# A sixth buffer for split weights and six more 7-product row pairs in a decoder trunk

## The chip, the cores and the metric

The kernel runs on one core of one Trainium2 chip. The core has TensorE for matmuls (PE in the profile, with its weight loads shown apart as PEld), VectorE (DVE), ScalarE (ACT), GpSimd (POOL) and SyncE (SP, which here only issues transfers). The metric is the device time of one execution in microseconds, the median of several runs; lower is better.

## The reference

The model is a trunk of two layers over 256 tokens of width 2048. The first layer is RetNet retention with 8 heads, the second DeepSeek-style latent attention with 16 heads on one shared key and value; each is followed by an MLP with a squared ReLU and an inner width of 8192. Everything is float32.

```python
def sq_relu_mlp(h, w1, w2):
    return jnp.square(jax.nn.relu(h @ w1)) @ w2

x = x + retention(rms_norm(x, norm_mix[0]), ...)
x = x + sq_relu_mlp(rms_norm(x, norm_mlp[0]), mlp_w1[0], mlp_w2[0])
k_nope, k_pe, v = mla_shared_kv(rms_norm(x, kv_norm_in), ...)
x = x + mla_attention(rms_norm(x, norm_mix[1]), ..., k_nope, k_pe, v, ...)
x = x + sq_relu_mlp(rms_norm(x, norm_mlp[1]), mlp_w1[1], mlp_w2[1])
```

The weights of the two MLPs are four matrices of 64 MB each, more than half of all that is read.

## The kernel before

**Split products.** TensorE multiplies a rounded float32 form. To keep the precision, each operand is split into a high part (`wh` for weights, a cast on ScalarE, line 216) and a low part (`wl`, a subtraction on VectorE, line 217), and one product of blocks is three matmuls: high x high, high x low, low x high (lines 409 to 411). So every weight passes through ScalarE and VectorE before TensorE can use it. High and low parts have 5 buffers each, of 1024 columns.

**Row pairs and column pairs.** The matrices of the MLPs, the output projections and most of retention's are read in pieces of 1 MB, each a 2x2 of blocks: 256 rows (a row pair) by 1024 columns (a column pair). `gemm_pair` walks over the 8 row pairs of one column pair and adds into PSUM; `quad` does one row pair. A row pair is multiplied in one of two ways, chosen by the list `kinds`:

- with 8 products (the plain way): two high and two low parts of 1024 columns;
- with 7 products (a Strassen-Winograd form): VectorE first makes three sums u1 to u4 of the weight blocks (lines 363, 372 and 373), and then the blocks b11, b22, b21 and the sums are split into four high and four low parts, one of them half as wide. The activation side needs sums too, made by `with_sums` (lines 451 to 460) and held in a second activation tile, `more`. The sums of the results come out in `pair_out`.

The raw weights lie in 3 buffers (`raw`). A load is issued by SP as soon as the last reader of a buffer is done. In a row pair of 7 the last reader of the raw weights is the low part of b21, the second of its four low parts.

**The MLP.** `mlp` goes through 4 groups of 2048 hidden columns. A group has two column pairs of w1 (tiles `u_...`, results through `up`: ReLU, transposes on TensorE, square, split, and `with_sums` for 4 of its 8 hidden blocks) and two column pairs of w2 (tiles `d_...`). Results of w2 of groups 0 to 2 are added to x in device memory: `to_home` issues 8 accumulating transfers of 256 KB from GpSimd's queue, spaced out over the next column pair. The last group brings x back. Which row pairs have 7 products: in the first column pair of w1 of groups 1 to 3 it is `ODD` (1, 3, 5, 7), in the second `SEVEN` (3, 5, 7); in w2 `SEVEN` and then `ODD`.

**Order.** Program order comes from a queue: `later(n, fn)` puts work off by n ticks (one tick is one row pair), and `queued_behind` fixes the order of two instructions on their engine. The compiler's scheduler orders the rest, so an instruction can be issued before an earlier one of the program that waits for more. Each engine then issues its own list strictly in order, and waits on semaphores. Tiles come from pools with a fixed number of buffers for a tag; a tile whose buffers are all in use waits for the last reader of one. The activation tiles (`act`, 24 buffers) are all in use in a group: 12 of the layer's input (8 blocks and 4 `more`), 12 of the hidden blocks.

## Time and profile before

| | us |
|---|---|
| median of 3 runs | 2459.61 (2458.16 to 2460.76) |
| the profiled execution | 2458.1 |
| its span, from the first to the last instruction | 2456.3 |
| PE busy, PEld busy | 2446.2, 2057.6 |
| DVE busy | 2212.2 |
| ACT busy | 1641.3 |
| POOL busy | 238.0 |

The granted TensorE clock is 1.00 over the whole span. The first MLP runs from 721 to 1402 us, the second from 1774 to 2452 us. Matmuls overlap, so that each shows about 0.39 us of length while they start about 0.23 us apart; TensorE's pace is read from starts and counts, not from lengths. In the rows of the profile a group is named by line, engine, operation and its tiles, output<-input, with the numbers of tiles left out. "Idle before" is the time the engine stood still ahead of an instruction, with what ended that time.

### The profile page before, as it was taken

Reading aid. Unit: us, or ns where it says so; the run is one execution under the profiler, and the core shown is the slowest. Engines: PE = TensorE matmul, PEld = TensorE weight load, DVE = VectorE, ACT = ScalarE, POOL = GpSimd, SP = SyncE. Lnnn points to the kernel's source line nnn. Section 1 sums busy time; section 2 is a strip of 40 time slices with the busy share of each in tenths; the row PEclk is TensorE's granted clock in tenths of the full one; section 3 lists DMA queues with packets and bytes.
Section 4 is the critical chain, followed back from the end, with each engine's and each line's share of the span. In section 5 each row is a group of like instructions: output and inputs, shape, how many; then the busy total and the mean of one; then the engine's idle time right before and its main releaser. Section 6 shows DMA issues by size and latency. Waiting matters only on the chain.

```text
span 2456.3 us, 31721 instructions
## 1 busy us (share of the span) xinstructions
PE 2446.2 (100%) x11614; PEld 2057.6 (84%) x11614; DVE 2212.2 (90%) x2919; ACT 1641.3 (67%) x2307; POOL 238.0 (10%) x287
## 2 busy tenths in 40 slices
PE   9999999999999999999999999999999999999999
PEld 7888888888888888888888888998888888888887
DVE  7899899888899999999999998777899999999998
ACT  6566666556676767667676777577667667676674
POOL 6400001000000010010110001101000100100100
PEclk9999999999999999999999999999999999999999
DMA  8555569556565586695786555444555865957854
GB/s 309 207 201 191 192 202 259 191 183 224 197 218 194 196 254 218 207 272 187 241 253 213 200 202 180 155 162 173 197 199 205 252 228 194 262 198 229 264 209 170
DMA packets 93692, 521.05 MB, mean 212 GB/s; under 512 B 11104, under 2 KB 12512, under 8 KB 40288
## 3 DMA queue, kind: packets, MB, share of 16 engines
q1 hardware_dynamic: 72144, 472.83, 55.2%
q0 software_dynamic: 21248, 46.15, 8.9%
q8 instruction: 91, 1.49, 0.2%
q14 instruction: 65, 0.53, 0.1%
q10 hardware_dynamic: 144, 0.05, 0.0%
HBM read 479.14 MB, written 39.85 MB: 211 GB/s over the span
## 4 chain that ended last, share of the span: by engine, by line
PE 92%; DVE 2%; ACT 1%; issue 0%; DMA 0%; POOL 0%; ACTq 0%; DVEq 0%
PE u_c L411 7%; PE u_c L410 7%; PE u_c L409 7%; PE d_c L411 6%; PE d_c L410 6%; PE d_c L409 6%; PE rp_c L411 3%; PE rp_c L409 3%; PE rp_c L410 3%; PE u_p L411 2%; PE u_p L410 2%; PE u_p L409 2%; PE rq_acc L307 2%; PE rk_acc L307 2%; PE ro_c L411 2%; PE ro_c L409 2%
## 5 line engine op out<-in xcount | busy, mean ns | idle before, releaser
L217 DVE TENSOR_TENSOR d_wl<-d_raw,d_wh 128x1024 fp32r<-128x1024 f32 (+1 forms) x256 | 278.7, 1111 | 31.6 <-ACT d_wh L216 31.6
L217 DVE TENSOR_TENSOR u_wl<-u_raw,u_wh 128x1024 fp32r<-128x1024 f32 (+1 forms) x256 | 279.3, 1113 | 29.8 <-ACT u_wh L216 29.8
L409 PE MATMUL u_c<-u_wh,n 128*128 128x512 f32 x712 | 278.3, 392 | 0.0
L411 PE MATMUL u_c<-u_wh,n 128*128 128x512 f32 x712 | 277.2, 389 | 0.0
L410 PE MATMUL u_c<-u_wl,n 128*128 128x512 f32 x712 | 277.2, 389 | 0.0
L409 PE MATMUL d_c<-d_wh,hid 128*128 128x512 f32 x706 | 275.4, 392 | 0.5 <-ACT d_wh L216 0.5
L411 PE MATMUL d_c<-d_wh,hid 128*128 128x512 f32 x706 | 275.0, 390 | 0.0
L410 PE MATMUL d_c<-d_wl,hid 128*128 128x512 f32 x706 | 274.8, 389 | 0.0
L216 ACT CAST u_wh<-u_raw 128x1024 fp32r<-128x1024 f32 (+1 forms) x256 | 241.3, 973 | 49.6 <-PE u_c L411 24.1
L216 ACT CAST d_wh<-d_raw 128x1024 fp32r<-128x1024 f32 (+1 forms) x256 | 240.3, 971 | 39.9 <-PE d_c L411 16.6
L216 ACT CAST d_wh<-d_u 128x1024 fp32r<-128x1024 f32 x106 | 108.1, 1051 | 119.7 <-DVE d_u L373 82.6
L216 ACT CAST u_wh<-u_u 128x1024 fp32r<-128x1024 f32 x104 | 106.2, 1052 | 116.0 <-DVE u_u L373 77.3
L411 PEld LDWEIGHTS u_c<-u_wh,n 128*128 128x128 f32 x712 | 133.7, 188 | 27.8
L410 PEld LDWEIGHTS u_c<-u_wl,n 128*128 128x128 f32 x712 | 133.8, 188 | 27.4 <-DVE u_wl L217 0.3
L409 PEld LDWEIGHTS u_c<-u_wh,n 128*128 128x128 f32 x712 | 133.7, 188 | 27.0
L409 PEld LDWEIGHTS d_c<-d_wh,hid 128*128 128x128 f32 x706 | 132.6, 188 | 28.2 <-ACT d_wh L216 1.4
L411 PEld LDWEIGHTS d_c<-d_wh,hid 128*128 128x128 f32 x706 | 132.5, 188 | 27.6
L410 PEld LDWEIGHTS d_c<-d_wl,hid 128*128 128x128 f32 x706 | 132.6, 188 | 27.5 <-DVE d_wl L217 0.4
L216 ACT CAST rp_wh<-rp_raw 128x1024 fp32r<-128x1024 f32 x112 | 103.8, 945 | 74.2 <-PE rp_c L411 49.2
L217 DVE TENSOR_TENSOR rp_wl<-rp_raw,rp_wh 128x1024 fp32r<-128x1024 f32 x112 | 119.7, 1090 | 16.4 <-ACT rp_wh L216 16.2
L217 DVE TENSOR_TENSOR u_wl<-u_u,u_wh 128x1024 fp32r<-128x1024 f32 x104 | 123.5, 1222 | 3.1 <-ACT u_wh L216 2.8
L217 DVE TENSOR_TENSOR d_wl<-d_u,d_wh 128x1024 fp32r<-128x1024 f32 x106 | 125.8, 1221 | 0.0
(570 smaller groups left out, 6505.3 us busy)
## 6 DMA issues: line engine op xcount, KB each, us to landing
u_raw<-in_mlp_w SPq DMA_DIRECT2D x128, 1024.0 KB, 5.4
d_raw<-in_mlp_w SPq DMA_DIRECT2D x128, 1024.0 KB, 4.9
rp_raw<-in_ret_w_gv SPq DMA_DIRECT2D x56, 1024.0 KB, 4.8
ro_raw<-in_ret_w_out SPq DMA_DIRECT2D x32, 1024.0 KB, 4.9
uq_raw<-in_mla_w_uq SPq DMA_DIRECT2D x24, 768.0 KB, 4.3
rq_raw<-in_ret_w_qk SPq DMA_DIRECT2D x16, 1024.0 KB, 4.9
rk_raw<-in_ret_w_qk SPq DMA_DIRECT2D x16, 1024.0 KB, 4.8
xh<-d_c POOLq DMA_DIRECT2D x48, 256.0 KB, 6.1
```

Source lines behind the costliest of these rows:

```text
L216: nc.scalar.copy(h, src)
L217: return nc.vector.tensor_tensor(l, src, h.bitcast(F32), op=ALU.subtract)
L307: nc.tensor.matmul(acc[f], wh[:, cols], a.rearrange("p i s -> p (i s)"), start=k == 0, stop=k == nk - 1)
L409: nc.tensor.matmul(dst, ah, bh, start=n == 0, stop=False)
L410: nc.tensor.matmul(dst, ah, bl, start=False, stop=False)
L411: nc.tensor.matmul(dst, al, bh, start=False, stop=n == total[key] - 1)
```

## The change

- The high and the low parts get 6 buffers each.
- In groups 1 to 3 of both MLPs the first column pair of w1 has 5 row pairs with 7 products (`FIVE`: 1, 3, 5, 6, 7), taken in the order 0, 1, 3, 2, 5, 4, 6, 7. The sums of activation block 6, which nothing held so far, are made again from its high and low part by `sum_again`, during the second column pair of w2 of the group before, and held in a `more` tile.
- The space comes from several places: in a row pair of 7, u2 and u4 are summed in place in the raw weights, so that one `us` buffer is left of two; the parts of u1 and u3 now come before those of u2 and u4; the mask is cut to two blocks; the rope frequencies and gains come by loads of their own into a shared buffer when they are needed, not with the constants; the rope tables and the rotated key share two buffers; `small` has 26 buffers, not 36.

```diff
-            wh = pool.tile([P, 1024], F32R, tag="wh", bufs=5, name=f"{name}_wh{half}")
-            wl = pool.tile([P, 1024], F32R, tag="wl", bufs=5, name=f"{name}_wl{half}")
+            wh = pool.tile([P, 1024], F32R, tag="wh", bufs=6, name=f"{name}_wh{half}")
+            wl = pool.tile([P, 1024], F32R, tag="wl", bufs=6, name=f"{name}_wl{half}")
...
-        u = [pool.tile([P, 2, 512], F32, tag="us", bufs=2, name=f"{name}_u{i}") for i in range(2)]
+        u = pool.tile([P, 2, 512], F32, tag="us", bufs=1, name=f"{name}_u")
...
-        nc.vector.tensor_tensor(u[1][:, 0], u[0][:, 0], raw[:, 512:1024], op=ALU.add)
-        summed_up = nc.vector.tensor_tensor(u[1][:, 1], u[1][:, 0], raw[:, 1536:], op=ALU.add)
+        summed_up = nc.vector.tensor_tensor(raw[:, 1024:1536], u[:, 0], raw[:, 512:1024], op=ALU.add)
         b11, b22 = parts(raw[:, 0:1024], 2, 0, summed_up)
         mm("p1", a(0, 0), b11)
         mm("c12", s(3), b22)
         (b21,) = parts(raw[:, 1536:], 1, 1, summed_up)
         mm("c11", a(0, 1), b21)
-        u2, u4 = parts(u[1].rearrange("p i n -> p (i n)"), 2, 2)
+        last_sum = nc.vector.tensor_tensor(raw[:, 1536:], raw[:, 1024:1536], raw[:, 1536:], op=ALU.add)
+        queued_behind(last_sum, low_part[0])
+        u1, u3 = parts(u.rearrange("p i n -> p (i n)"), 2, 3, last_sum)
+        mm("p5", s(1), u1)
+        mm("p7", s(0), u3)
+        u2, u4 = parts(raw[:, 1024:], 2, 2)
         mm("c21", a(1, 1), u4)
         mm("p6", s(2), u2)
-        u1, u3 = parts(u[0].rearrange("p i n -> p (i n)"), 2, 3)
-        mm("p5", s(1), u1)
-        mm("p7", s(0), u3)
...
-    rope_tab = pool.tile([P, 2, S], F32, name="rope_tab")
-    pe_tabs = [[pool.tile([P, 2, ROPE], F32, name=f"petab{t}{i}") for i in range(2)] for t in range(NT)]
+    rope_tab = pool.tile([P, 2, S], F32, tag="tab", bufs=2, name="rope_tab")
+    pe_tab = pool.tile([P, NT, 2, 2, ROPE], F32, tag="tab", bufs=2, name="pe_tab")
+    pe_tabs = [[pe_tab[:, t, i] for i in range(2)] for t in range(NT)]
...
+    def inverse(lo, n, name):
+        inv = f2k([n], name)
+        nc.sync.dma_start(inv, a["cst"][:, lo : lo + n])
+        return inv
+
     def mla_tables():
+        gpe = f2k([2 * ROPE], "gpe")
+        nc.sync.dma_start(gpe, a["gpe"])
...
-        ret_sc.append(sincos(cst[:, C_INVR : C_INVR + 128], 128, "tr"))
+        ret_sc.append(sincos(inverse(C_INVR, 128, "invr"), 128, "tr"))
...
-            nc.sync.dma_start(cst, a["cst"])
-            nc.sync.dma_start(gpe, a["gpe"])
+            nc.sync.dma_start(cst, a["cst"][:, C_MASK:])
...
+        def sum_again(name):
+            v = act[6][0]
+            u = f2k([2, S], f"{name}_u")
+            nc.vector.tensor_tensor(u, v[:, :, 0].bitcast(F32), v[:, :, 1].bitcast(F32), op=ALU.add)
+            again[:] = [*act[:6], (v, with_sums(u, name)), act[7]]
...
-                seven = SEVEN if p % 2 else ODD if p else LATE
+                seven = SEVEN if p % 2 else FIVE if p else LATE
                 gemm_pair(
-                    w1, p * 8, act, [i in seven for i in range(8)], f"u{layer}_{p}", lambda c, p=p, up=up: up(c, p)
+                    w1, p * 8, again if p % 2 == 0 and p else act, [i in seven for i in range(8)], f"u{layer}_{p}",
+                    lambda c, p=p, up=up: up(c, p), order=(0, 1, 3, 2, 5, 4, 6, 7) if seven is FIVE else None,
                 )
...
+                if p and not last:
+                    later(4, lambda gi=gi: sum_again(f"n{layer}{gi}"))
+
```

More of the change, by code (lines that the diff above doesn't have):

```diff
@@ L47 @@
 SEVEN, LATE, ODD, HEAD = (3, 5, 7), (5, 7), (1, 3, 5, 7), (2, 4, 6, 7)
+FIVE = (1, 3, 5, 6, 7)
 QUERY, FOUR = (3, 4, 6, 7), (3, 5, 6, 7)
@@ L75, in small @@
     def small(w, name):
-        return pool.tile([P, w], F32, tag="small", bufs=36, name=name)
+        return pool.tile([P, w], F32, tag="small", bufs=26, name=name)
     def shaped(t, shape):
@@ L115, in yoco @@
     gains = pool.tile([P, G_ALL], F32, name="gains")
-    cst = pool.tile([P, C_ALL], F32, name="cst")
+    cst = pool.tile([P, C_ALL - C_MASK], F32, name="cst")
     pos_i = pool.tile([P, NT], I32, name="pos_i")
-    gpe = pool.tile([P, 2 * ROPE], F32, name="gpe")
     nc.scalar.dma_start(gains, a["gains"])
-    ident = cst[:, C_ID : C_ID + P]
-    mask = cst[:, C_MASK : C_MASK + 3 * P]
-    neg_half = pool.tile([P, 16], F32, name="neg_half")
+    mask = cst[:, 0 : 2 * P]
+    ident = cst[:, 2 * P : 3 * P]
+    neg_half = pool.tile([P, 8], F32, name="neg_half")
     nc.gpsimd.memset(neg_half, -0.5)
@@ L333, in parts @@
         def parts(src, n, part, after=None):
-            wh = pool.tile([P, 1024], F32R, tag="wh", bufs=5, name=f"{name}_wh{part}")
-            wl = pool.tile([P, 1024], F32R, tag="wl", bufs=5, name=f"{name}_wl{part}")
+            wh = pool.tile([P, 1024], F32R, tag="wh", bufs=6, name=f"{name}_wh{part}")
+            wl = pool.tile([P, 1024], F32R, tag="wl", bufs=6, name=f"{name}_wl{part}")
             low = low_part[0] = split(wh[:, : n * 512], wl[:, : n * 512], src)
@@ L695, in start @@
             later(6, scale_tables)
-            later(18, lambda: mla_sc.append(sincos(cst[:, C_INVM : C_INVM + 32], 32, "tm")))
+            later(18, lambda: mla_sc.append(sincos(inverse(C_INVM, 32, "invm"), 32, "tm")))
             later(26, mla_tables)
@@ L942, in yoco @@
     rc, ckv = [], []
-    kpe_t = pool.tile([P, 2, S], F32R, name="kpe_t")
+    kpe_t = pool.tile([P, 2, S], F32R, tag="tab", bufs=2, name="kpe_t")
     def downed(acc, b):
@@ L1225, in _constants @@
     causal = np.where(i[None, :] <= i[:, None], 0.0, -1e30)
-    cst[:, C_MASK : C_MASK + 3 * P] = np.concatenate([causal, np.zeros((P, P)), causal], axis=1)
+    cst[:, C_MASK : C_MASK + 2 * P] = np.concatenate([np.zeros((P, P)), causal], axis=1)
     cst[:, C_ID : C_ID + P] = np.eye(P)
```

7 lines of the change are left out of this document (4 added, 3 removed).

## The prediction

> **What bounds the kernel now.** I read the busy lines of the page first, then what TensorE waits for, then tables by stage, and last the timelines of VectorE and TensorE in one stage.
>
> ```profile
> span 2456.3 us, 31721 instructions
> PE 2446.2 (100%) x11614; PEld 2057.6 (84%) x11614; DVE 2212.2 (90%) x2919; ACT 1641.3 (67%) x2307; POOL 238.0 (10%) x287
> ```
> ```profile
> PE idle L131 <- DVE zeros L128: 1.2, 1, 1.2
> PE rg_acc L279 <- ACT a L218: 0.7, 1, 0.7
> ...
> PE d_c L409 <- ACT d_wh L216: 0.5, 2, 0.3
> ```
>
> TensorE is busy for 100% of the span, and its waits are tenths of a microsecond at a handful of places. VectorE is second with 90%. So one removed matmul is worth its full pace, and one added VectorE instruction is free only while VectorE stays ahead. The table by stage shows how far ahead. Its rows are one group of the first MLP: the second column pair of w2 of group 0 ("d, second"), the two column pairs of w1 of group 1 ("u, first" and "u, second"), and the first of w2 ("d, first"). Columns: window, its length, then busy time and instructions of PE, PEld, DVE, ACT and POOL, granted clock, DMA share, GB/s.
>
> ```profile
> 851.90:892.70 40.80, 40.80 (x181) 33.80 (x180) 37.49 (x41) 25.55 (x31) 6.96 (x8) 1.00 0.89 257
> 892.70:933.50 40.80, 40.80 (x181) 33.80 (x180) 37.06 (x41) 25.47 (x31) 6.90 (x8) 1.00 0.90 257
> 933.50:976.80 43.30, 43.30 (x201) 36.03 (x200) 40.95 (x52) 31.61 (x43) 0.00 (x0) 1.00 0.55 195
> 976.80:1020.10 43.30, 43.30 (x201) 36.04 (x200) 41.40 (x52) 31.62 (x43) 0.00 (x0) 1.00 0.55 194
> ```
>
> TensorE is never idle there, at clock 1.00. "u, first" has 4 row pairs of 7 products and 4 of 8, so (4x7 + 4x8) x 3 = 180 matmuls in 40.80 us: **0.227 us a matmul**. VectorE's idle time is 3.31, 3.74, 2.35 and 1.90 us, 11.30 us a group. What it waits for in this layer and in the second one (engine, line, us in total, times, longest):
>
> ```profile
> DVE u_wl L217 <- ACT u_wh L216: 10.4, 10, 1.8
> DVE u_u L363 <- DMA u_raw<-in_mlp_w: 4.0, 3, 2.0
> DVE d_u L363 <- DMA d_raw<-in_mlp_w: 3.9, 3, 2.1
> ```
> ```profile
> DVE u_u L363 <- DMA u_raw<-in_mlp_w: 2.1, 2, 1.5
> DVE d_u L363 <- DMA d_raw<-in_mlp_w: 0.3, 1, 0.3
> ```
> The timelines of VectorE, ScalarE and TensorE in "u, first" (start, length, instruction, idle before it):
> ```profile
> 889.72 1.23 DVE L217 TENSOR_TENSOR u_wl<-u_raw,u_wh 128x1024 fp32r<-128x1024 f32 x1 [1.57 <-ACT u_wh L216]
> ...
> 898.47 2.36 DVE L217 TENSOR_TENSOR u_wl<-u_u,u_wh 128x1024 fp32r<-128x1024 f32 x2
> 900.74 2.36 DVE L217 TENSOR_TENSOR u_wl<-u_raw,u_wh 128x1024 fp32r<-128x1024 f32 x2
> 903.01 1.22 DVE L363 TENSOR_TENSOR u_u<-u_raw 128x1024 f32<-128x1024 f32 x1
> ...
> 909.68 1.23 DVE L217 TENSOR_TENSOR u_wl<-u_raw,u_wh 128x1024 fp32r<-128x1024 f32 x1
> 912.91 1.23 DVE L363 TENSOR_TENSOR u_u<-u_raw 128x1024 f32<-128x1024 f32 x1 [2.01 <-DMA u_raw<-in_mlp_w]
> ...
> 927.00 2.35 DVE L217 TENSOR_TENSOR u_wl<-u_u,u_wh 128x1024 fp32r<-128x1024 f32 x2
> 930.51 1.23 DVE L217 TENSOR_TENSOR u_wl<-u_raw,u_wh 128x1024 fp32r<-128x1024 f32 x1 [1.16 <-ACT u_wh L216]
> ```
> ```profile
> 905.79 2.00 ACT L216 CAST u_wh<-u_u 128x1024 fp32r<-128x1024 f32 x2 [3.43 <-PE u_c L411]
> ```
> ```profile
> 900.41 0.39 PE L410 MATMUL u_c<-u_wl,n 128*128 128x512 f32 x1
> ...
> 932.37 0.39 PE L410 MATMUL u_p<-u_wl,n_more 128*128 128x512 f32 x1
> ```
> ```profile
> L217 DVE TENSOR_TENSOR u_wl<-u_u,u_wh 128x1024 fp32r<-128x1024 f32 x104 | 123.5, 1222 | 3.1 <-ACT u_wh L216 2.8
> ```
>
> Three readings. (1) VectorE's lead over TensorE is small: the first of the two low parts from 898.47 lasts 1.22 us, ends at 899.69 and is used at 900.41 (lead 0.72 us); the second of the two from 927.00 ends at 929.35 and is used at 932.37 (3.02 us). (2) Part of its idle time is a full buffer: the 1.57 us before 889.72 end with a ScalarE cast, and such casts wait for TensorE to free a high part (the 3.43 us before 905.79). (3) The rest is weights that land late: 2.01 us before 912.91.
>
> **The change part by part.**
>
> *Fifth row pair of 7 products.* Six column pairs (2 layers, groups 1 to 3) lose one product of 3 matmuls: 18 x 0.227 = **-4.08 us**. On VectorE a row pair of 8 costs two low parts, 903.01 - 900.74 = 2.27 us; one of 7 costs three sums and four low parts, 909.68 - 903.01 = 6.67 us. The swap adds 4.40 us of VectorE per column pair, which itself becomes 0.68 us shorter.
>
> *Sums of row pair 6, made again* (one 512-wide sum, the three of `with_sums`, a cast and a low part), in "d, second" of each group before:
>
> ```profile
> L373 DVE TENSOR_TENSOR u_u<-u_u,u_raw 128x512 f32<-128x512 f32 x4 | 2.8, 690 | 0.1
> ```
> ```profile
> L455 DVE TENSOR_TENSOR hid_sum<-hid_u x32: 418/422/429, 773.6 to 2379.4; 128x256 f32<-128x256 f32 x32
> ```
> ```profile
> L456 DVE TENSOR_TENSOR hid_sum<-hid_sum,hid_u x32: 284/292/297, 775.1 to 2381.6; 128x128 f32<-128x128 f32 x32
> ```
>
> The third of `with_sums` and the low part have the widths of the second and of the 512-wide sum: 0.69 + 0.42 + 0.29 + 0.29 + 0.69 = 2.38 us of VectorE. It has 3.31 us idle in that stage, so I put it at nothing; without that cover it costs up to 2.38 us x 6 = 14.3 us. Its cast goes to ScalarE, idle for 15.25 of the 40.80 us. The 25th activation tile that it needs takes the place of a hidden block that "d, second" has read by then; no wait expected.
>
> *Does VectorE still keep up?* A group had 11.30 us idle; 4.40 + 2.38 + 0.68 = 7.46 go, and 3.84 us stay. In the two critical stages in a row ("d, second", "u, first") 7.05 us were idle and 7.46 are wanted: 0.41 us too few, to be taken from the lead. If late weights stay as late as now, they take (4.0 + 3.9) / 3 = 2.6 us a group more in the first layer, and 0.8 us in the second. So the lead must give 0.4 to 3.0 us per group, and is rebuilt in the two stages after, which keep 4.25 us idle less what the next item takes.
>
> *Sixth buffer of high and low parts.* It gives room of one part, 6 to 12 matmuls, 1.36 to 2.72 us: what VectorE idles for a full buffer (1.57 us before 889.72) becomes lead. With the smallest lead shown, 0.72, some 2.1 to 3.4 us can be given. That covers 0.4 and 0.8 + 0.4, and 3.0 only with the larger gain. I price the stalls of the six stages at **0**, with bounds 0 and 2.3 us per group (the second case in the rivals).
>
> *New order inside every row pair of 7*: u1 and u3 go to TensorE before u2 and u4, which are now summed in place in the weights' own buffer. VectorE does the same three sums. Two prices are not in the trace. First, the last sum is now followed by its cast and only one low part covers that cast: cast 1.00 us of the 2.00 us pair at 905.79 plus two hand-overs against a low part of 1.13, so between 0 and about 0.2 us of VectorE per row pair; I take 0.05, since the next row pair's first sum can be put there, and up to 9 x 0.2 = 1.8 us in the two critical stages for the range. Second, the weights' buffer is freed only after the last low part, two low parts or 2.3 us later than now, and loads of "u, first" already land late.
>
> ```profile
> u_raw<-in_mlp_w SPq DMA_DIRECT2D x128, 1024.0 KB, 5.4
> ...
> xh<-d_c POOLq DMA_DIRECT2D x48, 256.0 KB, 6.1
> ```
>
> A load takes 5.4 us at the median, beside eight 256 KB accumulating transfers of POOL in each critical stage (DMA share 0.89 to 0.90 against 0.55 in the other two). Three weight buffers leave a load the time of two row pairs, 2.27 + 6.67 = 8.9 us at VectorE's full pace, so the median load is in time and a doubly shared one is not. I keep the waits as they are now; lower bound none, upper 2.0 us in each of the 12 critical stages.
>
> *What a sixth buffer may do elsewhere.* TensorE idles a little near the ends of both MLPs and in the projections between:
>
> ```profile
> 1356.40:1402.00 45.60, 44.98 (x203) 36.19 (x202) 44.65 (x65) 31.80 (x52) 2.44 (x5) 1.00 0.51 182
> 1402.00:1431.00 29.00, 28.52 (x212) 27.59 (x212) 21.78 (x46) 22.94 (x53) 3.80 (x6) 1.00 0.64 224
> 1431.00:1474.00 43.00, 42.76 (x193) 34.90 (x192) 42.36 (x62) 30.15 (x47) 2.20 (x1) 1.00 0.59 207
> ...
> 2409.00:2452.00 43.00, 42.29 (x184) 33.98 (x182) 41.50 (x51) 19.55 (x23) 0.00 (x0) 1.00 0.48 159
> ```
>
> 0.62 + 0.48 + 0.24 + 0.71 = 2.05 us idle. VectorE is nearly full there (44.65 of 45.60), so more room helps only with what was done ahead; bounds 0 and -2.05, I take half: **-1.0**.
>
> *Space made for it.* The constants' load is split: the frequencies come by a load of their own just before the tables, the rope gains much later. POOL starts its chain for the tables later by the landing of that load; bounds 0 and one load of 5.4 us:
>
> ```profile
> 18.15 1.55 POOL L570 TENSOR_SCALAR tr_ang<-cst,pos_f 128x128 f32<-128x128 f32 x2 [17.31 <-DVE pos_f L628]
> ...
> 59.55 0.73 POOL L206 TENSOR_TENSOR n_r<-n_m,neg_half 128x2 f32<-128x2 f32 x1 [1.89 <-DVE n_m L205]
> ```
>
> The chain ends with 1.89 us to spare, and the table is copied only at 72.9:
>
> ```profile
> L641 ACT COPY rope_tab<-tr_tp x1: 581/581/581, 72.9 to 72.9; 128x512 f32<-128x512 f32 x1
> ```
> So nothing, up to 3 us if the cover goes. The gains' load sits on SP behind weight loads, and the VectorE instructions that read it hold back those queued behind them; one load of 5.4 us at most, where the lead is not yet needed; nothing. Fewer small tiles and shared table buffers: nothing; if a reuse must wait, the late reader is a small reduction on VectorE.
>
> **Sum.** -4.08 - 1.0 + 0 = -5.1 us. The profiled execution took 2458.1 us, 1.8 more than its span; 2458.1 - 5.1 = 2453.0. The median of the runs, 2459.6, is 1.5 above the profiled one: **2454.5 us**, ratio 0.998.
>
> **Rivals.**
> - *The products go, and nothing more* (B): no stall is recovered elsewhere, and up to 1.1 us per group is lost where the lead is short. 2459.6 - 4.1 = 2455.5, and up to 2462; middle 2457.5. For it: 0.72 us of lead, and VectorE as full as 98% where the idle time of TensorE lies. Against it: the full-buffer waits of 10.4 us in ten places, which a buffer removes.
> - *Late weights make VectorE the bound in the critical stages* (C, slower): weight buffers are freed 2.3 us later, so each of the 12 critical stages waits 2.0 us; 4.0 + 0.41 us per group against 2.1 us of lead (0.72 and the buffer's smaller gain, 1.36) leaves 2.3 x 6 = 13.8 us of stalls: 2459.6 - 4.1 + 13.8 = 2469. It decides from 1.5 us per group, where 9.0 us of stalls turn -4.1 into +4.9. For it: the first layer has six such waits in its six critical stages, the longest 2.0 and 2.1 us. Against it: the second layer waits 2.4 us in all, with the same code.
> - *VectorE bounds the whole kernel* (D, slower): each added VectorE microsecond counts, 6 x (4.40 + 2.38) = 40.7 us, 2459.6 - 4.1 + 40.7 = 2496. For it: 90% busy. Against it: TensorE has no idle time in the four windows, and VectorE waits for buffers that TensorE frees.
>
> The Trainium skill, "Perfetto Trace Analysis", section "Identifying the Most-Contended Engine", says to judge TensorE by the busy share of its weight loads, not of its matmuls, and to take the engine of highest occupancy as the one to optimise. By that rule the 84% of PEld stand below VectorE's 90%, and the case is D. The trace does not bear it out before the change: the gaps are on VectorE's side.
>
> **How the numbers follow.** Forecast 0.40 (own range 2452.5 to 2455.5), B 0.32, C 0.24, D 0.04. The measurement tells about 0.2% (4.9 us) from no change. The forecast lies just beyond it, B within, C and D above: faster 0.40, same 0.32, slower 0.28. The range runs from 2452.5 (all 2.05 us recovered and one more of run spread) to 2467, into the middle of C's stalls.
>
> **What would show it.** Right: matmuls 18 fewer; no idle TensorE in the shortened "u, first", now 40.1 us; VectorE busy there for some 41 us less what it did ahead; its waits for casts nearly gone. Wrong: TensorE waiting for `u_wl` or `u_wh`, VectorE waiting for weights in both critical stages of both layers, or TensorE idle before the end of the first rope.

## The result, and the profile after

The changed kernel takes **2481.8 us** (median, 2479.9 to 2484.0) where the kernel before took 2459.6: ratio **1.0089**, 95% interval 1.0075 to 1.0103. The forecast was 2454.5 and the range ended at 2467, so the change is slower where a small gain was forecast. The page of the changed kernel:

```profile
span 2480.0 us, 31816 instructions
PE 2451.3 (99%) x11596; PEld 2055.1 (83%) x11596; DVE 2260.7 (91%) x2979; ACT 1643.2 (66%) x2325; POOL 250.3 (10%) x287
```

The 18 matmuls are gone (11596 against 11614), and VectorE has 48.5 us more work. The span is 23.7 us longer. Set the first matmul of each stage in the two traces against each other, and the difference grows like this: +4.87 us up to the first MLP; +1.77, +2.29, +5.21, +2.86, +2.34 and +6.37 us in the two column pairs of w1 of groups 1 to 3 of the two layers (20.84 together); -2.0 in all the rest. The removed matmuls are in the 20.84 already, so the six groups hold 20.84 + 4.08 = 24.9 us of new stalls. The table by stage of the changed kernel, group 1 of the first MLP (the four stages that the prediction showed):

```profile
856.83:897.63 40.80, 40.80 (x181) 33.78 (x180) 39.53 (x46) 25.96 (x32) 6.92 (x9) 1.00 0.89 257
897.63:937.80 40.17, 40.17 (x179) 33.27 (x178) 39.44 (x43) 25.55 (x32) 6.17 (x8) 1.00 0.84 234
937.80:983.48 45.68, 43.73 (x200) 35.76 (x199) 42.28 (x53) 32.34 (x44) 0.00 (x0) 1.00 0.59 210
983.48:1026.78 43.30, 43.30 (x200) 35.91 (x199) 42.93 (x54) 31.14 (x43) 0.78 (x1) 1.00 0.53 193
```

"u, first" is 40.17 us, down from 40.80, with no idle time: that pair does what it was built for. The loss is in the *next* stage, "u, second", 45.68 us where it was 43.30, though it has as many products as before. What TensorE waits for longest in the MLPs and outside them, in the changed kernel (us in total, times, longest):

```profile
PE hid_tp L235 <- ACT u_c L893: 16.9, 8, 3.3
PE rp_c L410 <- DVE rk_u L712: 1.2, 2, 1.0
```
What the casts of ScalarE wait for, before and then after:

```profile
ACT u_wh L216 <- DMA u_raw<-in_mlp_w: 5.9, 5, 2.0
```
```profile
ACT u_wh L216 <- DMA u_raw<-in_mlp_w: 28.6, 22, 2.7
```

In the MLPs TensorE does not wait for weights or VectorE, but for the ReLU (line 893): at the start of "u, second" it transposes the results of "u, first", which pass through ScalarE first. And the casts on ScalarE wait 28.6 us for weights that have not landed; before it was 5.9 us in five waits. The timeline of ScalarE around the worst of these places shows how the two belong together. Before, group 3 of the first MLP:

```profile
1270.03 1.10 ACT L216 CAST u_wh<-u_raw 128x1024 fp32r<-128x1024 f32 x1
1270.98 0.77 ACT L877 ACTIVATE u_c<-u_c,n_r 128x512 f32<-128x512 f32 x1
1271.60 2.99 ACT L216 CAST u_wh<-u_raw 128x1024 fp32r<-128x1024 f32 x3
1274.44 2.22 ACT L877 ACTIVATE u_c<-u_c,n_r 128x512 f32<-128x512 f32 x3
```

After, the same place:

```profile
1280.65 2.00 ACT L216 CAST u_wh<-u_raw 128x1024 fp32r<-128x1024 f32 x2 [0.53 <-DMA u_raw<-in_mlp_w]
1282.56 0.72 ACT L893 ACTIVATE u_c<-u_c,n_r 128x512 f32<-128x512 f32 x1
1285.54 1.04 ACT L216 CAST u_wh<-u_raw 128x1024 fp32r<-128x1024 f32 x1 [2.27 <-DMA u_raw<-in_mlp_w]
1286.49 0.72 ACT L893 ACTIVATE u_c<-u_c,n_r 128x512 f32<-128x512 f32 x1
1287.12 0.60 ACT L216 CAST u_wh<-u_raw 128x512 fp32r<-128x512 f32 x1
1287.63 1.33 ACT L893 ACTIVATE u_c<-u_c,n_r 128x512 f32<-128x512 f32 x2
```

ScalarE issues its list in order. The four ReLUs stand between casts for the next column pair, in both kernels. Before, the three casts between the first and second ReLU ran without a wait. After, the cast at 1285.54 stands 2.27 us for its weights with three ReLUs behind it, and TensorE stands with them. Written out from the two compiled lists (the number is the row pair that a cast belongs to, counted from 0; `out` are the copies of `pair_out`):

```
before: ...                          out out out out cast1 | ReLU  cast1 cast2 cast2  ReLU  ReLU  ReLU
after:  cast0 cast0 out cast1 out cast1 out out out cast2 cast2 | ReLU  cast3  ReLU  cast3  ReLU  ReLU
```

After the change, two casts of the *fourth* row pair (cast3) are ahead of the last ReLUs; before, none is. There are three raw buffers, so the load for the fourth row pair cannot go out before the first row pair of the same column pair has been split.

The two traces also say when that load comes. It goes out at about the same point of "u, second" in both kernels: 0.3 us ahead of the stage's first matmul before, between 0.8 us ahead of it and 0.9 us behind it after. It lands 4.5 to 7.5 us behind that matmul before (mean 5.7) and 6.6 to 9.3 us after (mean 7.6). Before, the four ReLUs start 1.2, 4.6, 5.5 and 6.1 us behind it in all six groups; in group 3 of the two layers the load lands at 7.2 and 7.5 us, behind all of them, and costs nothing. After, the second ReLU starts 7.7 to 10.3 us behind it. So the load is 1.9 us later on average, and the cast that needs it has moved ahead of the ReLUs.

### The profile page after: what moved, and what is told of

The parts are those of the page before. It is cut to its first block, busy times and chain, and to the rows that moved or that the text cites. A ratio compares the mean times of both kernels' runs of the same rounds, so it can differ in the third digit from the quotient of the medians.

```text
span 2480.0 us, 31816 instructions
## 1 busy us (share of the span) xinstructions
PE 2451.3 (99%) x11596; PEld 2055.1 (83%) x11596; DVE 2260.7 (91%) x2979; ACT 1643.2 (66%) x2325; POOL 250.3 (10%) x287
## 4 chain that ended last, share of the span: by engine, by line
PE 79%; DVE 11%; DMA 4%; issue 3%; ACT 3%; POOL 0%; SPq 0%; ACTq 0%; DVEq 0%
PE d_c L410 6%; PE d_c L412 6%; PE d_c L411 6%; PE u_c L412 4%; PE u_c L410 4%; PE u_c L411 4%; DMA u_raw<-in_mlp_w 3%; DVE u_wl L217 3%; PE rp_c L410 3%; PE rp_c L412 3%; PE rp_c L411 3%; PE rq_acc L307 2%; PE ro_c L412 2%; PE ro_c L410 2%; PE ro_c L411 2%
## 5 line engine op out<-in xcount | busy, mean ns | idle before, releaser
L216 ACT CAST u_wh<-u_raw 128x1024 fp32r<-128x1024 f32 (+1 forms) x314 | 294.5, 973 | 162.4 <-DVE u_raw L378 98.8
L216 ACT CAST d_wh<-d_raw 128x1024 fp32r<-128x1024 f32 (+1 forms) x309 | 292.7, 982 | 119.4 <-DVE d_raw L378 75.5
L217 DVE TENSOR_TENSOR d_wl<-d_raw,d_wh 128x1024 fp32r<-128x1024 f32 (+1 forms) x309 | 341.5, 1127 | 20.2 <-PE u_c L410 13.5
L217 DVE TENSOR_TENSOR u_wl<-u_raw,u_wh 128x1024 fp32r<-128x1024 f32 (+1 forms) x314 | 342.2, 1120 | 17.7 <-ACT u_wh L216 10.0
L410 PE MATMUL u_c<-u_wh,n 128*128 128x512 f32 x676 | 266.3, 394 | 0.4 <-ACT u_c L433 0.4
L412 PE MATMUL u_c<-u_wh,n 128*128 128x512 f32 x676 | 265.5, 393 | 0.0
L216 ACT CAST rp_wh<-rp_raw 128x1024 fp32r<-128x1024 f32 (+1 forms) x140 | 133.4, 965 | 113.0 <-PE rp_c L412 59.6
L217 DVE TENSOR_TENSOR rp_wl<-rp_raw,rp_wh 128x1024 fp32r<-128x1024 f32 (+1 forms) x140 | 153.8, 1119 | 14.7 <-ACT rp_wh L216 13.6
L152 POOL DMA_DIRECT2D xh<-d_c x48 | 41.7, 868 | 781.6 <-ACT d_c L433 617.6
L410 PE MATMUL rp_c<-rp_wh,a 128*128 128x512 f32 x280 | 109.7, 392 | 1.2 <-DVE rk_u L712 1.2
L412 PE MATMUL rp_c<-rp_wh,a 128*128 128x512 f32 x280 | 109.2, 390 | 0.0
L411 PE MATMUL rp_c<-rp_wl,a 128*128 128x512 f32 x280 | 109.0, 389 | 0.0
```

Of the source, the lines that this page charges most:

```text
L152: ins = nc.gpsimd.dma_start(x_home[t][2 * p + j], c[t][j][i], accum_op=ALU.add)
L216: nc.scalar.copy(h, src)
L217: return nc.vector.tensor_tensor(l, src, h.bitcast(F32), op=ALU.subtract)
L410: nc.tensor.matmul(dst, ah, bh, start=n == 0, stop=False)
L411: nc.tensor.matmul(dst, ah, bl, start=False, stop=False)
L412: nc.tensor.matmul(dst, al, bh, start=False, stop=n == total[key] - 1)
```

## The experiments

The theories behind the first runs: **F**, the fifth row pair overfills VectorE and ScalarE at the end of its column pair. **O**, the sixth buffer lets the compiler list parts of the next column pair ahead of the ReLU. **W**, weights are late because the sums in place hold a raw buffer longer, and a cast waits for them ahead of the ReLU. None was right alone; a fourth, **L**, came from the later runs: the harm is a cast of the fourth row pair listed ahead of a ReLU, *times* the lateness of that row pair's weights. Each part of the change by itself moves such a cast ahead of a ReLU (fifth_alone, six_high, no_fifth_five_bufs).

All runs are given with the ratio to the kernel before on the same chip and its 95% interval. "Six groups" is the difference to the kernel before over the six groups, worked out as above; a kernel with the fifth row pair and no stalls would have -4.08. The last two columns come from the one profiled execution of each kernel, which lay within 2.4 us of the median time, but 4.6 us above it in no_fifth.

| kernel | us | ratio | up to the first MLP | six groups |
|---|---|---|---|---|
| changed | 2481.8 | 1.0089 (1.0075 to 1.0103) | +4.87 | +20.84 |
| no_fifth | 2478.1 | 1.0075 (1.006 to 1.009) | +5.16 | +20.72 |
| fifth_alone | 2467.7 | 1.003 (1.0017 to 1.0042) | +0.70 | +7.00 |
| relu_first | 2464.7 | 1.0021 (1.0012 to 1.003) | +3.94 | +4.47 |
| five_bufs_four_raw | 2464.2 | 1.0016 (1.0007 to 1.0026) | +2.08 | +7.00 |
| five_bufs | 2484.8 | 1.0097 (1.0079 to 1.0115) | +1.36 | +25.04 |
| no_fifth_five_bufs | 2470.8 | 1.0042 (1.0027 to 1.0056) | +3.06 | +10.79 |
| no_fifth_four_raw | 2458.7 | 0.9993 (0.9984 to 1.0002) | +1.97 | +0.31 |
| relu_first_no_fifth | 2467.7 | 1.0031 (1.0012 to 1.005) | +3.04 | +7.67 |
| six_high | 2468.1 | 1.0032 (1.0023 to 1.0042) | +2.78 | +6.20 |
| own_sums | 2484.8 | 1.0098 (1.0085 to 1.0112) | +3.00 | +25.25 |
| own_sums_relu | 2460.8 | 1.0005 (0.9996 to 1.0014) | +3.21 | +0.58 |
| five_bufs_relu | 2472.3 | 1.005 (1.0033 to 1.0067) | +3.10 | +11.95 |
| fifth_order | 2460.5 | 1.0 (0.9991 to 1.0009) | +2.16 | +1.11 |
| own_sums_order | 2484.8 | 1.0101 (1.0085 to 1.0116) | +7.96 | +17.52 |
| four_raw_order | 2466.8 | 1.0025 (1.0015 to 1.0036) | +2.47 | +7.63 |
| four_raw_order_b | 2467.6 | 1.0029 (1.0017 to 1.004) | +2.19 | +8.96 |
| fifth_sum_pool | 2477.3 | 1.0069 (1.0053 to 1.0084) | +0.70 | +8.37 |
| own_sums_relu_third | 2465.3 | 1.002 (1.0011 to 1.003) | +3.45 | +3.19 |

### Which part of the change

**no_fifth**: the changed kernel without the fifth row pair.

```diff
-                seven = SEVEN if p % 2 else FIVE if p else LATE
+                seven = SEVEN if p % 2 else ODD if p else LATE
...
-                if p and not last:
+                if False:
```

> The changed kernel without the fifth row pair: 4 row pairs of 7 in natural order in the first column pair of groups 1 to 3, and no sums made again; six buffers, sums in place and the space-making stay. The 18 removed matmuls come back (4.1 us). Theory F (the fifth row pair fills VectorE and ScalarE at the end of the column pair, so that the ReLU comes late): the stalls at the start of 'u, second' go; 2481.8 - 24.9 + 4.1 = 2461. Theory O (the sixth buffer lets parts of the next column pair be listed ahead of the results' chain of pair_out and ReLU): they stay; 2481.8 + 4.1 = 2486. Theory W (weights come late, because the sums in place hold their buffer longer, and a cast that waits for them stands ahead of the ReLU): they stay in part, since the rows of 7 are farther apart; 2470 to 2486.

Measured 2478.1. Its waits of TensorE:

```profile
PE hid_tp L235 <- ACT u_c L893: 13.8, 8, 2.9
```

The waits for the ReLU stay, so F in its first form falls: the fifth row pair is not needed for them.

**fifth_alone**: the kernel before, with `FIVE`, its order and `sum_again` added (the last four pieces of the change's diff), and nothing else.

> The kernel before with the fifth row pair, its order and the sums made again, and nothing else: five buffers, sums in tiles of their own, no space-making. Theory F: the stalls come with it; 2459.6 - 4.1 + 24.9 = 2480. Theory O: no sixth buffer, no stalls; 2455.5. Theory W: the weights' buffer is free as early as before; 2455.5 to 2460.

Measured 2467.7, slower than every number that O and W gave (2455.5 to 2460). The stalls of 11.1 us (7.00 + 4.08) are of another kind:

```profile
PE u_c L410 <- ACT u_wh L217: 5.2, 6, 0.9
PE u_p L411 <- DVE u_wl L218: 1.8, 2, 1.1
```

Here TensorE does wait for parts of weights: once a group, for the high part of the third row pair of "u, first". So the fifth row pair costs more than its products give, without any other part of the change.

**relu_first**: the changed kernel with one edge more. `queued_behind` puts the first cast of the fourth row pair behind the last ReLU of the column pair before.

```diff
+                if hold[0] is not None:
+                    hold[1] -= 1
+                    if hold[1] == 0:
+                        queued_behind(last_cast[0], hold[0])
+                        hold[0] = None
...
-                        nc.scalar.activation(c[t][i], c[t][i], AF.Relu, scale=r[t])
+                        hold[:] = [nc.scalar.activation(c[t][i], c[t][i], AF.Relu, scale=r[t]), 3]
```

> The changed kernel with one edge of order more, on ScalarE: the first cast of the 4th row pair of a column pair is listed behind the last ReLU of the column pair before. No data or buffer changes. If the late weights do their harm only through the cast ahead of the ReLU (the page's 1.19 and 2.27 us before such casts), as theories W and O have it: the starts of 'u, second' lose most of their 16.9 us of waits for the ReLU, and the time falls to about 2481.8 - 17 = 2465. Theory F in its form that VectorE is simply too full: the wait moves to u_wl or u_wh, and the time stays within 5 us of 2481.8.

Measured 2464.7, 17.1 us less than the changed kernel, as O and W gave it; no data, buffer or product is different.

```profile
PE hid_tp L236 <- ACT u_c L899: 5.2, 9, 0.7
```

The waits for the ReLU fall from 16.9 to 5.2 us. The load of the fourth row pair lands as late as in the changed kernel (mean 7.7 us behind the stage's first matmul, 7.6 there), so it is not the lateness alone that costs. In the six groups the edge moves the two casts behind the ReLUs on ScalarE; a few sums of hidden blocks also change places on VectorE, behind the first transposes. That the order of the lists carries most of the loss is shown by this run.

**five_bufs_four_raw** and **five_bufs**: the changed kernel with 5 high and low buffers, and with 4 or 3 raw buffers.

```diff
-wh ... tag="wh", bufs=6
-wl ... tag="wl", bufs=6
-raw ... tag="raw", bufs=3
+wh ... tag="wh", bufs=5
+wl ... tag="wl", bufs=5
+raw ... tag="raw", bufs=4   (five_bufs keeps 3)
```

> The changed kernel with 5 high and low buffers, and 4 buffers of raw weights in place of 3. The fifth row pair, its order and the sums in place stay. Theory W: a load is issued one row pair earlier, VectorE's and ScalarE's waits for weights go, and with them the stalls; 2455 to 2460. Theory O: no sixth buffer, no stalls, the same 2455 to 2460. Theory F: 2480, since the work at the end of the column pair is the same.

> The changed kernel with 5 high and low buffers in place of 6, and nothing else undone. Theory O (the sixth buffer changes the order of the lists and so delays the ReLU): the waits for the ReLU at the start of 'u, second' go, and what is left is near the run with five buffers and four raw ones, 2464 to 2467. Theory W (weights late through the sums in place, with 3 raw buffers): the waits for weights and some of the stalls stay; 2470 to 2480.

Measured 2464.2 and 2484.8. O gave 2455 to 2460 for the first and, with that run known, 2464 to 2467 for the second; W gave 2470 to 2480 for the second, so five_bufs is above both. Without the sixth buffer the time does not come back, and O falls as the only cause. In the six groups the two kernels have the same lists on ScalarE and VectorE; only the fourth raw buffer tells them apart, and it is worth 18.0 us there (25.04 against 7.00). With three raw buffers, ScalarE and TensorE:

```profile
ACT u_wh L216 <- DMA u_raw<-in_mlp_w: 28.7, 19, 2.7
```
```profile
PE u_p L411 <- DVE u_wl L217: 7.0, 9, 1.2
PE u_c L410 <- ACT u_wh L216: 3.5, 6, 0.6
PE hid_tp L235 <- ACT u_c L893: 3.4, 5, 2.4
```

With four:

```profile
ACT u_wh L216 <- DMA u_raw<-in_mlp_w: 2.4, 2, 1.6
```
```profile
PE u_c L410 <- ACT u_wh L216: 3.5, 6, 0.6
```

The late weights are real, and the fourth buffer removes them: the load of the fourth row pair goes out 3.0 us earlier and lands 4.4 us earlier on average. What stays is mostly the 3.5 us for `u_wh` ahead of the third row pair of "u, first", as in fifth_alone; both have +7.00 in the six groups, though not spread over them alike.

**no_fifth_five_bufs** and **no_fifth_four_raw**: the space-making alone (sums in place, the new order of parts), five buffers, four row pairs of 7, with 3 and with 4 raw buffers.

> Only the space-making of the change: sums in place, u1 and u3 ahead of u2 and u4, one us buffer, constants by loads of their own; five buffers, 4 row pairs of 7. Theory O: no stalls in the MLPs; the kernel before and 1 to 2 us for the start of the first layer, 2460 to 2462. Theory W: weights freed later are late in the MLPs too; 2465 to 2478.

> The space-making of the change, 5 high and low buffers, 4 raw buffers, no fifth row pair: the run with five buffers and no fifth row pair (2470.8), with one raw buffer more. Theory W (the sums in place hold a raw buffer longer, and with three the next loads are late): the 14 us of stalls in the six groups go, 2470.8 - 10.8 = 2460, within 2 us. If three raw buffers were enough and the new order of parts itself costs the time: no change, 2470.

Measured 2470.8 and 2458.7. The first:

```profile
PE hid_tp L235 <- ACT u_c L893: 4.6, 3, 2.9
```

Again the lists in the six groups are the same (each has one cast3 ahead of the third ReLU), and the fourth raw buffer takes 10.79 us of stalls to 0.31. So W holds for this part of the change: the sums in place, with the new order of parts, cost 10.8 us with three raw buffers and nothing with four. It also shows that a cast3 ahead of a ReLU is harmless when its weights are there. The second kernel is the quickest of all runs, but its interval includes 1.

**relu_first_no_fifth**: the edge of relu_first and no fifth row pair, six buffers.

> Six buffers and the space-making, no fifth row pair, and the 4th row pair's first cast behind the last ReLU. Theory O: the 20.7 us of stalls in the six groups of the run without the fifth row pair go but for about 1 us each; 2478 - 15 = 2463. If the stalls that are left in the run with the ReLU first and the fifth row pair (0.8 to 2.3 us a group) come from the fifth row pair and not from the list's order, they go here: 2478 - 20.7 = 2457 to 2459.

Measured 2467.7, 10.4 us less than without the edge, but above both expectations, 2463 and 2457 to 2459. Four of the six groups lose nothing or 0.5 us, but group 3 of each layer 3.73 and 3.26. These are the groups in which x is also brought back in the same stretch. In the first layer's, 1.9 of the 3.73 us are two waits for the ReLU and 0.7 us two for copies of `pair_out`; the rest was not taken apart. The five runs of this kernel spread over 13.6 us, so its gain is the least certain of the four with this edge.

### The two factors

After these runs W was the leading theory, and its test was to undo the sums in place inside the changed kernel. **own_sums**: the changed kernel with u2 and u4 in a tile of their own and in the order of before; the space comes from the sixth low buffer (six high, five low). **six_high** is the same without the fifth row pair.

```diff
-        summed_up = nc.vector.tensor_tensor(raw[:, 1024:1536], u[:, 0], raw[:, 512:1024], op=ALU.add)
+        nc.vector.tensor_tensor(u[1][:, 0], u[0][:, 0], raw[:, 512:1024], op=ALU.add)
+        summed_up = nc.vector.tensor_tensor(u[1][:, 1], u[1][:, 0], raw[:, 1536:], op=ALU.add)
```

> The changed kernel with u2 and u4 summed in a tile of their own again and split ahead of u1 and u3, as before; the space comes from the sixth low buffer (six high, five low). The fifth row pair and its order stay. Theory W (the raw buffer, held longer by the sums in place, makes weights late, a cast waits for them and the ReLU behind it): the waits of casts for weights fall from 28.6 us to about the 10 us of the fifth row pair alone, the waits for the ReLU go, 2462 to 2468. If the sixth high buffer moves casts ahead of the ReLU and that alone does it (theory O): 2475 to 2482.

> The kernel before with a sixth high buffer and the space-making that it needs, but sums in tiles of their own; no fifth row pair, five low buffers. Theory W: weights in time, no stalls in the groups; 2458 to 2461, with up to 2 us recovered near the ends of the MLPs as in my prediction. Theory O: casts stand ahead of the ReLU here too; 2465 to 2478.

own_sums took 2484.8, above the numbers of W (2462 to 2468) and of O (2475 to 2482). This refutes W as the only cause as plainly as five_bufs refuted O. Its waits of TensorE, and ScalarE in group 2:

```profile
PE hid_tp L235 <- ACT u_c L892: 17.9, 6, 4.5
```
```profile
1109.08 1.07 ACT L216 CAST u_wh<-u_raw 128x1024 fp32r<-128x1024 f32 x1
1112.89 1.04 ACT L216 CAST u_wh<-u_raw 128x1024 fp32r<-128x1024 f32 x1 [2.75 <-DMA u_raw<-in_mlp_w]
1113.84 0.72 ACT L892 ACTIVATE u_c<-u_c,n_r 128x512 f32<-128x512 f32 x1
```

Its list has both cast3 ahead of the last ReLUs, as the changed kernel's has. six_high (2468.1) has one cast3 ahead of the second ReLU, and loses only in group 3 of the two layers (3.75 and 2.22; the other four groups 0.23 together). The load of the fourth row pair lands 5.8 and 5.9 us behind the stage's first matmul in those two groups and 3.2 to 3.8 us in the others. So a cast in the wrong place costs nothing while its weights are in time. This led to L, and to the run that tests it.

**own_sums_relu** and **five_bufs_relu**: own_sums and five_bufs with the edge of relu_first.

> The kernel with sums in tiles of their own, six high and five low buffers and the fifth row pair, and the first cast of the 4th row pair behind the last ReLU. With three raw buffers the load of the 4th row pair goes out only when the 1st has been split, so a ReLU behind its cast waits for a fresh load (theory L). Then the 17.9 us of waits for the ReLU go but for about 1 us a group, 2484.8 - 17 = 2468, near the fifth row pair alone (2467.7). If the ReLU is late for VectorE's sums ahead of it, not for the cast: above 2478.

> The changed kernel with five buffers, and the same edge. It has 3.4 us of waits for the ReLU and 12.7 us for u_wh and u_wl, with the first cast of the 4th row pair ahead of the 3rd ReLU. Theory L: 3 to 6 us go with the edge, 2479 to 2482, since the other stalls are parts that come late from late weights and a full VectorE, and only a fourth raw buffer cured them (2464.2). If all its stalls follow from the cast ahead of the ReLU: 2465.

own_sums_relu took 2460.8, **24.0 us less** than own_sums, more than the 17 that L gave, and no different from the kernel before. Its one edge takes the six groups from +25.25 to +0.58, though the load lands no earlier (mean 7.4 us, 7.2 in own_sums):

```profile
PE hid_tp L236 <- ACT u_c L898: 3.1, 4, 1.0
```

Why more than 17: the waits for the ReLU fall by 14.8 us, and 3.4 us of waits for `u_wl` go with them. The rest fits the clock: own_sums has three stretches at a granted clock of 0.50, 13.6 us in all, in which TensorE is busy for 12.3 us, and own_sums_relu has none in the groups. Half of 12.3 is 6.1 us, an estimate of what they cost (more on the clock at the end).

five_bufs_relu took 2472.3, 12.5 us less than five_bufs, where L gave 3 to 6 and its rival 19. So more of that kernel's stalls go with the edge than its 3.4 us of waits for the ReLU: its waits for `u_wl` fall too, from 9.2 to 1.6 us. L's direction holds, its size was off. In these two kernels the edge is less clean than in relu_first: the compiler also moves VectorE's sums for the fourth row pair behind work on the hidden blocks. How much of the gain comes from VectorE's list is not shown.

### What the fifth row pair gives

**fifth_order**: fifth_alone with `order=(0, 1, 2, 3, 5, 4, 6, 7)` in place of `(0, 1, 3, 2, 5, 4, 6, 7)`.

> The kernel before with the fifth row pair alone, in the order 0, 1, 2, 3, 5, 4, 6, 7 in place of 0, 1, 3, 2, 5, 4, 6, 7. It had one stall of 0.87 us ahead of the third row pair and 1.2 to 2.9 us in all in each of six groups. If two of 7 in a row there are the cause: 2467.6 - 7 = 2460 or below, down to 2456. If VectorE is overfilled whatever the order: 2467, within 2 us.

Measured 2460.5, the time of the kernel before. The two row pairs of 7 in a row at the start made the 0.87 us stall. What is left (1.11 + 4.08 = 5.2 us) has nearly no wait that shows: 0.6 us for `u_wl` in two places, and starts of matmuls some 0.1 us late. VectorE seems to hand over its parts at the last moment.

**own_sums_order**, **four_raw_order**, **four_raw_order_b**: the same order on own_sums and on five_bufs_four_raw, and on the latter the order `(0, 1, 2, 3, 5, 6, 4, 7)`.

> As the first of these, with the fifth row pair in the order 0, 1, 2, 3, 5, 4, 6, 7. If the order costs 7 us as it did with five buffers: 2456 to 2461, and at the lower end a version that is faster than the kernel before. If VectorE has nothing left in the groups, the order moves the stalls to many small ones: the time of the first of these less 2 to 4 us.

> The changed kernel with 5 high and low and 4 raw buffers, and the fifth column order 0, 1, 2, 3, 5, 4, 6, 7: no two row pairs of 7 in a row at the start of 'u, first', where the column pair before still has its results' sums on VectorE. If those two in a row make the stall of 0.59 us some 15 us into 'u, first' and what follows (1.6 us a group, 11.0 us in six): 2464.2 - 9 = 2455. If the fifth row pair overfills VectorE whatever the order: the stall moves to a later row pair, 2464, within 2 us.

> The same with the order 0, 1, 2, 3, 5, 6, 4, 7: three row pairs of 7 in a row in the middle, one of 8 ahead of the last. If VectorE's lead at the end of the column pair sets the stalls in 'u, second': 2455, or 1 us below the order 0, 1, 2, 3, 5, 4, 6, 7. If three of 7 in a row use up the lead: stalls of 1 to 2 us a group before row pair 6, 2462 to 2468.

Measured 2484.8, 2466.8 and 2467.6; none gained. With sums in place the stall moved from the third row pair to a later place (four_raw_order, 3.8 us in six waits for `u_wh`). That is the second case of four_raw_order, 0.8 us above its range, and of four_raw_order_b. own_sums_order took as long as own_sums, which neither of its cases had. In its profiled execution the six groups lose 7.7 us less than in own_sums, and 5.0 us more are lost up to the first MLP: a wait of 2.48 us for VectorE at 102.4 us, then 3.4 us at clock 0.50. The lists up to there are those of own_sums, so the new order did not make that loss; what did is not shown. An order that helps one form of the kernel need not help another.

**fifth_sum_pool**: fifth_alone with the sums of `sum_again` on GpSimd (`nc.gpsimd.tensor_tensor` for `nc.vector`).

> The kernel before with the fifth row pair alone, its sums made again on GpSimd in place of VectorE (the low part stays on VectorE, the cast on ScalarE). With the sums on VectorE each of the six groups had one stall of TensorE 12 us into 'u, first' (0.87 us before u_wh of the third row pair) and 1.2 to 2.9 us of stalls in all. If it is VectorE's 1.7 us of sums in 'd, second' that takes the lead: 2467.6 - 7 = 2460 or below. If it is the order of the row pairs, with two of 7 in a row: no change, 2467. If GpSimd is too slow, or slows VectorE: above 2468.

Measured 2477.3, 9.6 us more than with VectorE, the third case. The timelines show why. GpSimd:

```profile
854.26 1.63 POOL L873 TENSOR_TENSOR n_u<-n 128x512 f32<-128x512 f32 x1
855.96 1.07 POOL L457 TENSOR_TENSOR n_sum<-n_u 128x256 f32<-128x256 f32 x1
857.12 0.80 POOL L458 TENSOR_TENSOR n_sum<-n_sum,n_u 128x128 f32<-128x128 f32 x1
```

VectorE beside it:

```profile
853.61 0.68 DVE L373 TENSOR_TENSOR d_u<-d_u,d_raw 128x512 f32<-128x512 f32 x1
854.21 0.69 DVE L436 TENSOR_TENSOR d_u<-d_p,d_v 128x512 f32<-128x512 f32 x1
854.81 1.63 DVE L374 TENSOR_TENSOR d_u<-d_u,d_raw 128x512 f32<-128x512 f32 x1
856.37 1.22 DVE L439 TENSOR_TENSOR d_v<-d_p,d_v 128x512 f32<-128x512 f32 x1
```

A 512-wide sum takes VectorE 0.68 us, and 1.63 (line 374) or 1.22 us (line 439) while GpSimd works. Both read two tiles in SBUF, the on-chip memory of the pools; line 436, which reads one operand from PSUM, where the matmuls write, took 0.69 us beside GpSimd. In each of the six groups four of VectorE's instructions are slower, by some 2.0 us together, where 1.7 us of sums were taken off it: the work that was moved away came back on the engine that was to be relieved. The loss lies in the column pairs of w2, 8.8 us in the six groups, which the table's last column does not hold.

**own_sums_relu_third**: own_sums_relu with the first cast of the third row pair, too, behind the last ReLU (2 in place of 3 in the edge).

> As the kernel with sums in own tiles, six high buffers and the ReLU ahead of the fourth row pair's casts, but the first cast of the third row pair stands behind the last ReLU too. Theory L: the 3.1 us of waits for the ReLU (four of them, 0.58 to 1.01 us) go, and the groups give most of the 4.1 us of removed matmuls; 2460.8 - 3 = 2458, or 2456 with what follows such a wait. If the third row pair's parts then come late for TensorE, waits for u_wh or u_wl take their place: 2461 to 2465.

Measured 2465.3, 4.5 us more than own_sums_relu, the second case: the waits for the ReLU are down to 0.4 us, and others take their place:

```profile
PE u_p L416 <- DVE u_wl L218: 1.9, 3, 0.8
```

The edge also acts on "d, first", which follows a w1 pair, and the two w2 column pairs of a group, which had no stall before, are 0.4 us longer in most groups.

## Why the prediction was wrong

**Right.** The 18 matmuls and their pace (40.80 to 40.17 us is 0.63 against 0.68 forecast). VectorE's added work: a group's four stages rose from 156.9 to 39.53 + 39.44 + 42.28 + 42.93 = 164.2 us, 7.3 against 6.78 forecast. Some time recovered near the ends of the MLPs, where -1.0 was forecast: the ends gave 1.1 and 1.2 us, 2.3 together. Only the second is shown to be the sixth buffer's: there no kernel with five high buffers gains more than 0.3 us, and those with six gain 1.0 to 1.4 in all runs but one (0.7). At the end of the first MLP two kernels with five high and four raw buffers gain 0.8 and 0.9 us as well (no_fifth_four_raw, five_bufs_four_raw), so the gain there does not need the sixth buffer, and the forecast had it partly by luck.

**The step that failed** is the term "I price the stalls of the six stages at **0**", with at most 2.3 us per group: the six groups hold 24.9 us, 4.1 us each. It rested on VectorE's lead alone and on "I keep the waits as they are now", with upper bounds only for the 12 critical stages; the waits of casts for `u_raw` went from 5.9 to 28.6 us. Two things were missed. First, the price was sought on VectorE and in the stages with POOL's transfers; it was paid on ScalarE and in "u, second", which the prediction had counted among the stages that rebuild the lead. Second, the chain `pair_out`, ReLU, transposes was in no part of the prediction. It shares ScalarE's list with the casts, so any late cast that stands ahead of it stops TensorE, however large the lead of the parts is. In the changed kernel no wait of TensorE for `u_wh` or `u_wl` is listed at all, which the prediction had named as the sign of being wrong. The later freeing of the weights' buffer, which the prediction did weigh, is not needed for the loss: own_sums frees it as before and loses as much.

**The sixth buffer** was credited with lead alone. More buffers also let the casts stand earlier in the list. The runs show both: about 1 us recovered at the end of the second MLP, and cast3 ahead of a ReLU with six high buffers (own_sums, six_high), but with five and sums in place too (five_bufs, no_fifth_five_bufs), and in fifth_alone, where it costs no wait for the ReLU that is listed. How the compiler's scheduler comes to each list is not shown.

**The fifth row pair.** "0.41 us too few" was the right sum, but the stalls were put at 0; alone it costs 11.1 us in its order and 5.2 in the better one, for 4.08 us of products. It did not gain in any kernel that ran.

**Rival C** had late weights as its mechanism and 13.8 us as its price. The mechanism is half right: the weights are late, but TensorE waits for the ReLU, not for VectorE, and the six groups lose 24.9. **Rival D** gave 2496. VectorE's 91% did not decide here, since one edge on ScalarE, at 66%, gave back 17.1 us with VectorE's work the same. The Trainium skill, "Perfetto Trace Analysis", section "Identifying the Most-Contended Engine", would optimise the engine with the highest occupancy first. These runs do not agree: the gain came from the order of ScalarE's list, with VectorE as busy as before (2260.2 us in relu_first, 2260.7 in the changed kernel).

**Up to the first MLP** +0 was forecast and +4.87 came. Kernels with the code of before there (fifth_alone, fifth_sum_pool, fifth_order) show +0.70, +0.70 and +2.16, and own_sums_order is 5.0 us above own_sums with the same lists. So one profiled execution can differ by 2 us from another there, and once by 5. Steps of 1.8 to 2.0 us (the start of the third head's query stage) and 0.8 us stand in all four kernels with six high and six low buffers and in none with five low buffers. That the sixth buffers make them is likely; the wait behind them was not taken apart.

## What to carry to other kernels

An engine that serves both the inputs of the next stage and the outputs of the last one is a shared queue: ask what stands ahead of the output chain in its list, and whether each of those instructions can wait for a transfer. More buffers on one tag can let that list run ahead of the buffers of another tag (here three raw buffers), and then the wait that was harmless at the back of the list moves to the front. Before a buffer is added or its release put off, the cheap remedy is an order: one edge that keeps the output chain ahead of the parts that depend on the latest load was worth 10 to 24 us in the four kernels that got it. Set one row pair further ahead, the edge cost 4.5 us (own_sums_relu_third).

## What was not expected of the hardware

A long stall has a second price. The timeline of TensorE in group 3 of the first MLP, the changed kernel, and then the rows of the whole stage and of a stretch behind the gap:

```profile
1284.10 0.40 PE L411 MATMUL u_c<-u_wl,n 128*128 128x512 f32 x1
1287.27 1.12 PE L235 MATMUL hid_tp<-cst,u_c 128*128 128x128 f32 x4 [2.76 <-ACT u_c L893]
```
```profile
1278.20:1327.37 49.17, 46.41 (x201) 38.13 (x199) 41.95 (x53) 31.89 (x44) 2.46 (x5) 0.93 0.64 233
1289.00:1293.40 4.40, 4.40 (x12) 3.41 (x11) 3.37 (x7) 2.24 (x5) 0.00 (x0) 0.50 0.48 201
```

After 2.76 us of idle time TensorE's granted clock is 0.50. Twelve matmuls start in those 4.40 us, where 4.40 / 0.227 = 19 would. The clock is at 0.50 from 1286.54 to 1293.36 us, and once more in group 3 of the second MLP, from 2351.49 to 2354.91 us. TensorE is busy for 6.1 and 2.9 us of the two stretches; half of that, 4.5 us, is an estimate of their price. With the 16.9 us of waits for the ReLU it makes 21.4 of the 24.9 us; the rest was not taken apart.

The length of the gap alone does not decide. The first fall came 2.04 us into a gap of 2.76 us, and in six_high a gap of 1.89 us (1278.28 to 1280.17 us) was followed by 3.4 us at 0.50, while in the changed kernel a gap of 3.26 us (2004.97 to 2008.23 us) left the clock at 1.00. The Trainium skill, "TensorE: Matmul & The Clock Gate", section "What's actually happening", has TensorE at half rate after an idle window of about 3.4 us. By kind the trace agrees; the gaps of 2.76 and 1.89 us are shorter than that figure.

That VectorE's sums of two operands in SBUF slow down beside GpSimd's (0.68 to 1.63 us) was not expected either. The Trainium skill, "Perfetto Trace Analysis", section "Optimizing Scalar/DVE Operations", says that the two share a read port, so that moving work between them may not help; the run with the sums on GpSimd agrees, with 9.6 us lost.
